# Moving the single tile from the front of a row of blocks of three to its end (LayerNorm, affine and tanh-GELU on 8192 x 2048)

## The chip, the cores and the metric

One core of one Trainium2 chip. The metric is the device time of one execution in microseconds (us). A profile gives the span from the first to the last instruction, which is 1.7 us shorter than the time of the same execution (317.9 against 319.62 us in the kernel before).

## The reference

```python
def reference(x, gamma, beta, eps):            # x: 8 x 1024 x 2048, float32
    mean = np.mean(x, axis=-1, keepdims=True)
    var = np.var(x, axis=-1, keepdims=True)
    out = gamma * (x - mean) / np.sqrt(var + eps) + beta
    return 0.5 * out * (1 + np.tanh(np.sqrt(2 / np.pi) * (out + 0.044715 * out ** 3)))
```

The 8192 rows are 64 tiles of 128 rows; a tile is 1.049 MB. Each is read once and written once.

## The kernel before

64 is one more than 3 x 21. The kernel loads and stores tiles in blocks of three (3.1 MB a transfer) and computes their scales in groups of three, so a single tile has to stand somewhere. It stands at the front, as block 0 and group 0. Blocks decide the transfers, groups decide the order of statistics; in the code they are two separate lists.

```python
    R = 3; NB = 7                                  # tiles in a block, block buffers
    starts = [0] + list(range(1, ntiles, R))       # blocks: 1, 3, 3, ...
    ...
    def load(b):
        xt = xin.tile([P, R, d], F32, name="xt")   # always room for three tiles
        ...                                        # blocks 0 and 1: one DMA a tile; then one DMA a block
    for b in range(NB):
        load(b)                                    # seven blocks ahead, from SyncE's queue
    ...
    groups = [1] + [3] * ((ntiles - 1) // 3)       # first tile of each group of three: statistics on ScalarE,
    ...                                            # all others on VectorE
    def gelu(j):                                   # ScalarE, in place, then the store from ScalarE's queue
        ...
        elif q == dst.shape[1] - 1:                # last tile of its block (last three blocks: each tile by itself)
            nc.scalar.dma_start(out=dst, in_=blocks[b][:, :dst.shape[1], :])
            if b + NB < len(starts):
                load(b + NB)                       # into the buffer that this store frees
```

The other steps: per tile VectorE writes (x - mean) * gamma into PSUM (line 166), PE adds beta times the standard deviation (line 169), ScalarE takes the Gelu with the scale 1/std (line 178). GpSimd works out the scales, once per group.

## Time and profile before

| | before |
|---|---|
| time, median (range), 3 runs | 319.86 us (319.84 to 320.2) |
| span of the profiled run | 317.9 us |
| bytes moved | 134.38 MB |
| busy: VectorE, PE, ScalarE | 84%, 80%, 76% |

VectorE has the largest share among the engines.

### The profile page before, as it was taken

The numbers are of one execution on the slowest core, as the hardware profiler recorded it, in microseconds if no ns is written. First come the engines' busy times: TensorE is split into PE (matmuls) and PEld (weight loads), VectorE is DVE, ScalarE is ACT, GpSimd is POOL, SyncE is SP. The second block draws the span as 40 slices with busy tenths as digits, with TensorE's granted clock in tenths as the row PEclk, the third lists the DMA queues.
The fourth block names the chain that finished last, engine by engine and source line by source line (L and its number), as shares of the span: only waits on it lengthen the run. The fifth ranks groups of instructions, "written<-read, shape, count | busy, mean of one in ns | idle before, by whom it ended". The sixth has DMA issues, their size and how long they took to land.

```text
span 317.9 us, 2209 instructions
## 1 busy us (share of the span) xinstructions
PE 255.8 (80%) x528; PEld 104.1 (33%) x528; DVE 266.1 (84%) x344; ACT 242.6 (76%) x282; POOL 91.2 (29%) x181
## 2 busy tenths in 40 slices
PE   5987979978989889789789895777979595979920
PEld 2322434323433333333233332332423232424400
DVE  2678889999999999999999979797979879797600
ACT  2365989998898988988988969587787769685720
POOL 0203324414225144043142250404234150506000
PEclk9997979999999999999999999979799998979985
DMA  7999999999999999999999999999999999999996
GB/s 292 436 442 442 387 438 422 428 429 430 436 431 433 430 433 433 427 436 431 427 433 439 430 430 432 433 431 436 424 436 433 436 425 433 430 439 409 426 429 265
DMA packets 7649, 134.38 MB, mean 423 GB/s; under 512 B 850, under 2 KB 850, under 8 KB 1106
## 3 DMA queue, kind: packets, MB, share of 16 engines
q1 hardware_dynamic: 3456, 67.11, 49.5%
q10 hardware_dynamic: 4180, 67.13, 49.3%
q8 instruction: 4, 0.07, 0.1%
q14 instruction: 9, 0.07, 0.1%
HBM read 67.13 MB, written 67.11 MB: 422 GB/s over the span
## 4 chain that ended last, share of the span: by engine, by line
DMA 42%; DVE 31%; issue 9%; POOL 5%; PE 4%; ACT 4%; ACTq 0%; POOLq 0%; DVEq 0%; SPq 0%
DMA out_dram<-xt 26%; DVE ps L166 17%; DMA xt<-in_x_dram 16%; DVE st L125 13%; PE ps L169 4%; ACT xt L178 3%; DVE mv L127 1%; POOL y L149 1%; ACT w L160 1%; POOL t L152 1%; ACT junk L131 1%; POOL ve L148 1%; POOL t L151 1%; POOL y L153 1%; POOL t L150 0%
## 5 line engine op out<-in xcount | busy, mean ns | idle before, releaser
L169 PE MATMUL ps<-b_t,w 128*128 128x512 f32 x512 | 241.8, 626 | 44.4 <-DVE ps L166 38.9
L166 DVE SCALAR_TENSOR_TENSOR ps<-xt,mv,g_t 128x1024 f32<-128x1024 f32 x128 | 156.2, 1265 | 7.0 <-ACT xt L178 6.9
L169 PEld LDWEIGHTS ps<-b_t,w 128*128 128x128 f32 x512 | 99.0, 199 | 188.0 <-issue 102.3
L178 ACT ACTIVATE xt<-ps,y 128x1024 f32<-128x1024 f32 x128 | 137.3, 1104 | 25.9 <-PE ps L169 24.9
L125 DVE BATCH_NORM_STATS2 st<-xt 128x6 f32<-128x512 f32 x172 | 107.9, 680 | 23.3 <-DMA xt<-in_x_dram 23.3
L138 POOL TENSOR_SCALAR mv<-sq 128x1 f32<-128x1 f32 x21 | 8.7, 416 | 144.5 <-ACT junk L136 144.5
L136 ACT ACTIVATE junk<-xt,mv 128x2048 fp8e5<-128x2048 f32 x21 | 42.0, 2002 | 8.0 <-ACT xt L178 8.0
L131 ACT ACTIVATE junk<-xt 128x2048 fp8e5<-128x2048 f32 x21 | 40.0, 1904 | 8.4 <-DMA xt<-in_x_dram 7.9
L149 POOL TENSOR_TENSOR y<-ve,power 128x3 f32<-128x3 f32 (+1 forms) x22 | 34.7, 1577 | 1.8
L148 POOL TENSOR_SCALAR ve<-mv 128x3 f32<-128x3 f32 (+1 forms) x22 | 20.2, 918 | 45.5 <-DVE mv L127 45.3
L160 ACT ACTIVATE w<-ident,std 128x128 f32<-128x128 f32 x64 | 20.8, 388 | 7.1 <-POOL std L154 7.1
L127 DVE BATCH_NORM_AGGREGATE mv<-st 128x2 f32<-128x24 f32 x43 | 11.3, 263 | 2.7
L98 PE MATMUL ps<-g_t,ones 1*128 1x512 f32 x8 | 7.2, 1073 | 3.7 <-DMA g_t<-in_gamma_dram 3.7
L101 ACT ACTIVATE g_t<-ps 128x1024 f32<-128x1024 f32 x2 | 2.0, 1023 | 6.7 <-PE ps L98 6.7
L98 PE MATMUL ps<-b_t,ones 1*128 1x512 f32 x8 | 7.0, 1056 | 0.0
L152 POOL TENSOR_SCALAR t<-t 128x3 f32<-128x3 f32 (+1 forms) x22 | 6.3, 287 | 1.9
L151 POOL TENSOR_TENSOR t<-t,ve 128x3 f32<-128x3 f32 (+1 forms) x22 | 6.1, 276 | 1.7
L153 POOL TENSOR_TENSOR y<-y,t 128x3 f32<-128x3 f32 (+1 forms) x22 | 5.2, 235 | 1.8
L101 ACT ACTIVATE b_t<-ps 128x1024 f32<-128x1024 f32 x2 | 2.0, 1023 | 4.8 <-PE ps L98 4.8
L150 POOL TENSOR_TENSOR t<-y 128x3 f32<-128x3 f32 (+1 forms) x22 | 5.1, 234 | 1.7
L154 POOL TENSOR_TENSOR std<-ve,y 128x3 f32<-128x3 f32 (+1 forms) x22 | 4.3, 194 | 1.7
L98 PEld LDWEIGHTS ps<-g_t,ones 1*128 1x128 f32 x8 | 2.5, 325 | 6.8 <-issue 6.8
(12 smaller groups left out, 13.0 us busy)
## 6 DMA issues: line engine op xcount, KB each, us to landing
xt<-in_x_dram SPq DMA_DIRECT2D x20, 3072.0 KB, 22.5
out_dram<-xt ACTq DMA_DIRECT2D x18, 3072.0 KB, 34.9
out_dram<-xt ACTq DMA_DIRECT2D x9, 1024.0 KB, 18.3
xt<-in_x_dram SPq DMA_DIRECT2D x4, 1024.0 KB, 8.6
out_dram<-xt ACTq DMA_DIRECT2D x2, 512.0 KB, 12.1
g_t<-in_gamma_dram ACTq DMA_DIRECT2D x1, 8.0 KB
b_t<-in_beta_dram ACTq DMA_DIRECT2D x1, 8.0 KB
```

The source lines that it names most:

```text
L98: nc.tensor.matmul(pt[:, c:c + BANK], lhsT=ones[0:1, :], rhs=row[0:1, s.start + c:s.start + c + BANK], start=True, stop=True)
L125: nc.vector.bn_stats(out=sts[i][:, c, :], in_=xts[i][:, c * BANK:(c + 1) * BANK])
L127: nc.vector.bn_aggr(out=slot(i), in_=sts.pop(i))
L131: nc.scalar.activation(out=junk, in_=xts[i], func=ACTF.Identity, scale=-1.0 / d, accum_out=slot(i)[:, 0:1], saturate=False)
L136: nc.scalar.activation(out=junk, in_=xts[i], func=ACTF.Square, bias=slot(i)[:, 0:1], accum_out=sq, saturate=False)
L148: po.tensor_scalar(out=ve, in0=mvs[g][:, :, 1], scalar1=float(eps), scalar2=None, op0=ADD)
L149: po.tensor_tensor(out=y, in0=ve, in1=power[:, :m], op=mybir.AluOpType.pow)
L152: po.tensor_scalar(out=t, in0=t, scalar1=-0.5, scalar2=1.5, op0=MUL, op1=ADD)
L160: nc.scalar.activation(out=w, in_=ident, func=ACTF.Identity, scale=rstds[g][1][:, k:k + 1])
L166: nc.vector.scalar_tensor_tensor(out=pt, in0=xts[j][:, s], scalar=mvs[g][:, k, 0:1], in1=g_t[:, s], op0=ADD if j in on_scalar else SUB, op ...
L169: nc.tensor.matmul(pt[:, c:c + BANK], lhsT=wts[j], rhs=b_t[:, s.start + c:s.start + c + BANK], start=False, stop=True, skip_group_check=True)
L178: nc.scalar.activation(out=xts[j][:, s], in_=pt, func=ACTF.Gelu_apprx_tanh, scale=rstds[g][0][:, k:k + 1])
```

## The change

The intent: the row of blocks starts with full blocks of three and the single tile closes it; the groups likewise. The first loads ahead are then full buffers, and the last group is short.

```diff
-    starts = [0] + list(range(1, ntiles, R))
+    starts = list(range(0, ntiles, R))
...
-        m = R if i else 1
+        m = min(R, ntiles - i)
...
-            nc.sync.dma_start(out=xt, in_=src)
+            nc.sync.dma_start(out=xt[:, :m, :], in_=src)
...
-    groups = [1] + [3] * ((ntiles - 1) // 3)
+    groups = [3] * (ntiles // 3) + [1] * (ntiles % 3)
```

## The prediction

> **What bounds the kernel now.** I read the page from the top (busy shares, then the 40 slices), then the table of stretches, then the chain that ended last, then the single DMA issues. The 64 tiles are 128 rows of 2048 floats, 1.049 MB each way, so 128 tile transfers in all. The shares alone do not decide it: VectorE 84%, PE 80%, ScalarE 76%. The slices do:
>
> ```profile
> DVE  2678889999999999999999979797979879797600
> ...
> DMA  7999999999999999999999999999999999999996
> GB/s 292 436 442 442 387 438 422 428 429 430 436 431 433 430 433 433 427 436 431 427 433 439 430 430 432 433 431 436 424 436 433 436 425 433 430 439 409 426 429 265
> ```
>
> VectorE is full only from slice 6 to about slice 21 and has holes after that; the DMA row stands at 9 from the second slice to the last but one. A table of seven stretches that I cut at the events of the run (first store issued at 30.2, second at 44.5 and landed at 65.6, last load landed at 276.9, last store issued at 305.1; the last two columns are DMA share and GB/s) says the same in numbers:
>
> ```profile
> 0.00:30.20 30.20, 23.18 (x28) 8.83 (x29) 18.49 (x29) 12.84 (x16) 5.75 (x21) 0.97 0.95 399
> 30.20:44.50 14.30, 12.24 (x24) 5.05 (x23) 12.57 (x17) 12.87 (x15) 4.20 (x8) 0.86 1.00 415
> 44.50:65.60 21.10, 20.33 (x46) 8.33 (x44) 19.66 (x27) 19.42 (x23) 8.10 (x16) 0.98 1.01 426
> 65.60:138.00 72.40, 62.38 (x140) 25.51 (x140) 71.67 (x93) 64.10 (x76) 22.89 (x43) 1.00 1.00 432
> 138.00:276.90 138.90, 113.11 (x244) 46.29 (x243) 123.82 (x160) 112.36 (x131) 44.26 (x86) 0.96 1.00 432
> 276.90:305.10 28.20, 24.58 (x53) 10.14 (x51) 19.90 (x22) 20.98 (x24) 5.96 (x9) 0.94 1.00 425
> 305.10:317.90 12.80, 0.00 (x0) 0.00 (x0) 0.00 (x0) 0.00 (x0) 0.00 (x0) 0.62 0.78 328
> ```
>
> From these the span can be rebuilt. The page counts 134.38 MB; at 432 GB/s that is 311.1 us. What each stretch loses against 432: (432-399)/432 x 30.2 = 2.3 us at the start, 0.6 and 0.3 in the next two, none in the two long ones, 0.5 in the sixth, (432-328)/432 x 12.8 = 3.1 at the end. 311.1 + 6.8 = 317.9 us, the span to a tenth. The timed 319.86 us is 2.0 us more, outside the span. So the whole time is bytes, a start-up, and a drain; in the last 12.8 us no engine computes at all.
>
> The chain of waits must be read with this in mind. In the middle it runs along VectorE at 12.47 us for three tiles; near 133 us it leaves it, and then hops from store to load:
>
> ```profile
> 143.14 38.55 DMA out_dram<-xt
> 181.71 0.03 issue
> 181.74 22.47 DMA xt<-in_x_dram
> ...
> 209.48 44.87 DMA out_dram<-xt
> 254.37 0.03 SPq L70
> 254.40 0.03 issue
> 254.43 22.49 DMA xt<-in_x_dram
> ```
>
> A store of three tiles takes 45 us to land although its bytes need only 7.3 us at 432 GB/s: it stands behind two other stores and shares with the loads. A buffer comes free only then, and SyncE issues the next load within 0.1 us. The VectorE stretch is therefore no bound of the end: VectorE goes faster (12.47 us per three tiles) than the transfers can follow (2 x 3 x 1.049 MB / 432 GB/s = 14.6 us), and only piles up stores. The last step of the chain is ScalarE at 303.96 us, 14 us before the span ends, which is the drain again.
>
> **What the Trainium skill says.** "DMA: Bandwidth & Descriptors", section Specifications, gives 435 GB/s as the ceiling of the fabric and about 358 GB/s as a limit per core on the HBM side. The trace agrees with the first: 432 GB/s over 211 us. It contradicts the second for this run; "HBM Reference", section Specifications (TRN2), says why that may be: a core that streams alone is measured well above the share, at about 425 GB/s. Either way the transfers are at the ceiling. The section Issuing engines are not separate DMA queues of the first page says that transfers from ScalarE's and SyncE's queues run on the same 16 engines and interleave. The trace agrees: a three-tile load lands in 22.5 us with stores beside it, and in 7.3 us after the one before it when loads run alone (below). So what one queue does not use the other gets, and order alone takes no byte away.
>
> **The change part by part.** No instruction of weight is added or removed: 64 tiles, 43 with VectorE statistics, 21 with ScalarE's. The group of one goes from tile 0 to tile 63, and all other groups shift by one tile. Five effects:
>
> 1. Loads at the start. Blocks 0 and 1 are now both of three, so six single-tile loads instead of four, and the seven buffers take 21 tiles ahead instead of 19. Cost of issue: 0.44 us each (median), two more singles, against a queue that holds tens of us of work: 0 on the path.
>
> 2. The first tiles on the engines. Before, tile 0 is alone: statistics at 6.07, scale chain done at 11.18, stored at 30.17. After, tile 0 is one that ScalarE must pass over twice. ScalarE is free at 18.7 (the four evictions of gamma and beta), mean to 20.9, variance to 23.0; GpSimd's chain takes it to 27.1 (the trace has exactly this, for tile 1), diagonals to 28.1. This is the place that the first group of three, tiles 1 to 3, has now. It stores at 44.49. Without the Gelu of tile 0 in between, but with the next group's mean moved into the gap and a cold PE at the first matmuls, I get 43 to 45 for the store of tiles 0 to 2. So store k after stands where store k+1 stood before: compute is one tile behind, 12.47/3 = 4.2 us.
>
> 3. The first recycling. Before, the one-tile block's store frees a whole buffer and the eighth load goes out at 45.53. After, it waits for the first three-tile store. Single loads land at 13.80 (4 tiles), 21.12 (7), 28.42 (10): 2.44 us a tile. At 44.5, pure loads have brought 4 + 30.7/2.44 = 16.6 tiles; 4.4 are left, and with the three of the store 7.4 x 2.44 = 18.0 us of work, to 62.5. The second store (about 56.7) adds three tiles, to 69.8. The first store lands by 62.5 plus up to 2 or 3 us (the very first load took 5.26 us for 2.4 us of bytes), the eighth load is issued at 63 to 66 and moves by 68. The third store is issued at about 68.3. The queue is thus never empty, with 2 to 7 us to spare: cost 0, and a bubble of a few us if I am off.
>
> 4. The steady stretch: the same bytes at 432 GB/s. Loads issued later land later, but are needed later too; VectorE has 2.1 us per group in hand.
>
> 5. The end. All 64 loads are through by about 277 as before (the halves of the traffic stay equal), but the last is of one tile and the last group's chain is of one element per partition (2.25 us for tile 0 at the start, against 5.6 us for the last group now). From 277: statistics to 280, then four tiles at about 3.5 us of matmul, so the last Gelu near 295 to 300 in place of 305.1. At that time the queue holds more, 15 to 20 us of stores against 11.9. Stores also reuse eight completion counters in turn, so the last can't go out before the one eight earlier has landed; that one is the last three-tile store, at about 300. All this is under the drain: gain 0.
>
> Sum: 311.1 + 2.3 + 0.9 + 0.5 + 3.1 = 317.9 as before, plus an expected 0.1 us for part 3, plus 2.0 outside: 319.9 us.
>
> **Rivals.**
> (a) The bubble. The eighth load goes out some 18 us later; if the first store took 25 us to land rather than 18 to 21, and the second came late as well, the DMA row would show a hole near 62 to 70 and the time would be 321 to 324. For it: the one-tile store at 30.2 needed 15.3 us until the load that waits for it went out, so stores behind a queue of loads are slow. Against it: whatever makes the store slow is loads that move.
> (b) Compute bounds: then being one tile later at the front costs 4.2 us, 324. For it: the chain runs 85 us along VectorE. Against it: the DMA row, and 12.8 us of drain.
> (c) The tail bounds: an earlier last group would give up to 5 to 8 us, 312 to 315. For it: the chain ends in GpSimd, PE and ScalarE of the last group. Against it: 11.9 us between the last issue and its landing, in which the rate is 423 to 430 GB/s until 312.
> (d) A more even drain: in the last 4 us the rate falls to 203 and 16 GB/s. Other stores at the end could make this better or worse by 1 us.
>
> **Range and chances.** The core of the sum is bytes over a rate that neither part touches. (a) in a mild form and (d) make the spread: 318.5 to 322.0 us. 2% are 6.4 us: faster would need (c), slower (a) and (b) together. Faster 0.01, within 0.95, slower 0.04.
>
> **What would show it.** Right: the DMA row at 9 throughout, 134.38 MB, 432 GB/s in the middle; the first store, of 3072 KB, at 43 to 45; the eighth block's load at 63 to 66; the last store issued before 303 and more than 12 us in flight. Wrong: a slice of 7 or less near 60 to 72 (a); ScalarE's last Gelu within 5 us of the end (b); a span shortened by the amount that the last Gelu moves (c). The prediction as a whole falls if the rate in the middle is not 430 to 433, for which I see no reason.

## The result, and the profile after

| | before | after |
|---|---|---|
| time, median (range), 6 runs each | 320.2 us (319.84 to 320.26) | 320.3 us (319.98 to 320.85) |
| ratio, 95% interval | | 1.0009 (0.9996 to 1.0021) |
| span of the profiled run | 317.9 us | 318.3 us |
| first store issued | 30.17 us, one tile | 45.85 us, three tiles |
| load of the eighth block issued | 45.53 us | 62.95 us |
| last store issued | 305.11 us | 303.67 us |

A ratio here and below is the mean time of one kernel's fast runs over that of the other's of the same rounds, so not quite the ratio of the medians quoted. The times are the same within the noise: the interval contains 1.

First the slices of the changed kernel. The first store is 16 us later, yet the DMA row has no hole: 9 from the second slice to the last but one.

```profile
DVE  0675688999999999999999999999797979899300
...
DMA  7999999999999999999999999999999999999995
```

Then the same seven stretches (columns as in the prediction: busy time and count of PE, weight load, VectorE, ScalarE and GpSimd, the granted clock, DMA share, GB/s).

```profile
0.00:30.20 30.20, 16.09 (x19) 6.15 (x20) 15.74 (x25) 12.12 (x14) 5.04 (x14) 1.00 0.96 398
30.20:44.50 14.30, 12.59 (x25) 5.17 (x25) 9.35 (x12) 10.09 (x14) 4.30 (x8) 1.00 0.99 423
44.50:65.60 21.10, 18.97 (x43) 7.73 (x42) 19.48 (x25) 19.34 (x22) 8.31 (x13) 1.00 1.01 428
65.60:138.00 72.40, 62.38 (x140) 25.22 (x138) 71.58 (x94) 64.61 (x77) 22.25 (x45) 1.00 1.00 431
138.00:276.90 138.90, 115.58 (x252) 47.33 (x251) 129.72 (x168) 117.57 (x138) 44.66 (x87) 0.97 1.00 432
276.90:305.10 28.20, 25.34 (x56) 10.60 (x54) 19.99 (x23) 18.73 (x20) 11.37 (x15) 0.95 1.00 425
305.10:318.30 13.20, 0.00 (x0) 0.00 (x0) 0.00 (x0) 0.00 (x0) 0.00 (x0) 0.57 0.74 309
```

In the first 30.2 us VectorE works 15.7 us instead of 18.5 and PE 16.1 instead of 23.2: compute really starts later. The last column hardly moves. Against 432 GB/s the changed kernel loses 0.4 us less than before in the two stretches from 30.2 to 65.6, 0.2 us more from there to 138, and 0.7 us more in the last one, where no engine computes in either kernel.

The most telling place is 60 to 64 us. These are the two queues there (SyncE's loads are q1, ScalarE's stores q10; packets, each one piece of a transfer that one DMA engine moves, MB, share of the 16 engines), in the kernel before and then after.

```profile
q1 hardware_dynamic: 40, 0.98, 57.0%
q10 hardware_dynamic: 43, 0.69, 40.2%
```

```profile
q10 hardware_dynamic: 83, 1.65, 95.8%
q1 hardware_dynamic: 1, 0.00, 0.0%
```

After the change the loads ahead are used up at 60 us and the next load is not yet on its way. The loads stand still. The stores that are waiting take their place at once, and the sum of the two queues (1.67 and 1.65 MB) is the same.

Last, the shares of the chain that ended last. In the kernel before:

```profile
DMA 42%; DVE 31%; issue 9%; POOL 5%; PE 4%; ACT 4%; ACTq 0%; POOLq 0%; DVEq 0%; SPq 0%
```

and after:

```profile
DVE 51%; DMA 20%; issue 12%; PE 6%; ACT 3%; POOL 3%; ACTq 0%; DVEq 0%; POOLq 0%; SPq 0%
```

From "mostly DMA" to "mostly VectorE", at equal time. The chain follows back from the last Gelu, and the last Gelu does not end the kernel: it ends 13 to 15 us before the span does. What moved is the place where the chain leaves VectorE for a store and the load behind it (near 133 us before, near 197 after), not a bound. The traces also show when the compute has used up its stock of loaded tiles: from 30 us on, VectorE waits for no load until 189.69 us before and 228.03 us after; from then on it waits some 2 us for a load in every group, and the groups come every 14.5 us, the pace of the transfers, in place of 12.47.

### The profile page after: what moved, and what is told of

Same layout as the page of the kernel before. It is cut to its first block, busy times and chain, and to the rows that moved or that the text cites. A ratio compares the mean times of both kernels' runs of the same rounds, so it can differ in the third digit from the quotient of the medians.

```text
span 318.3 us, 2212 instructions
## 1 busy us (share of the span) xinstructions
PE 251.0 (79%) x528; PEld 102.2 (32%) x528; DVE 265.8 (84%) x344; ACT 242.5 (76%) x282; POOL 95.9 (30%) x181
## 2 busy tenths in 40 slices
DMA packets 7649, 134.38 MB, mean 422 GB/s; under 512 B 850, under 2 KB 850, under 8 KB 1106
## 4 chain that ended last, share of the span: by engine, by line
DVE 51%; DMA 20%; issue 12%; PE 6%; ACT 3%; POOL 3%; ACTq 0%; DVEq 0%; POOLq 0%; SPq 0%
DVE ps L166 29%; DVE st L125 20%; DMA out_dram<-xt 13%; DMA xt<-in_x_dram 7%; PE ps L169 6%; DVE mv L127 2%; ACT xt L178 2%; POOL t L151 1%; POOL t L152 1%; ACT junk L131 1%; POOL y L149 1%; ACT w L160 0%; POOL mv L138 0%; POOL ve L148 0%; POOL y L153 0%
## 5 line engine op out<-in xcount | busy, mean ns | idle before, releaser
L169 PE MATMUL ps<-b_t,w 128*128 128x512 f32 x512 | 237.0, 616 | 48.1 <-DVE ps L166 35.7
L169 PEld LDWEIGHTS ps<-b_t,w 128*128 128x128 f32 x512 | 97.1, 195 | 188.7 <-issue 97.8
L149 POOL TENSOR_TENSOR y<-ve,power 128x3 f32<-128x3 f32 (+1 forms) x22 | 35.6, 1616 | 1.8
L148 POOL TENSOR_SCALAR ve<-mv 128x3 f32<-128x3 f32 (+1 forms) x22 | 21.1, 959 | 38.8 <-DVE mv L127 38.5
L151 POOL TENSOR_TENSOR t<-t,ve 128x3 f32<-128x3 f32 (+1 forms) x22 | 8.2, 375 | 1.7
L152 POOL TENSOR_SCALAR t<-t 128x3 f32<-128x3 f32 (+1 forms) x22 | 7.1, 321 | 1.9
L154 POOL TENSOR_TENSOR std<-ve,y 128x3 f32<-128x3 f32 (+1 forms) x22 | 5.2, 238 | 1.7
L153 POOL TENSOR_TENSOR y<-y,t 128x3 f32<-128x3 f32 (+1 forms) x22 | 4.3, 194 | 1.8
```

Of the source, the lines that this page charges most:

```text
L148: po.tensor_scalar(out=ve, in0=mvs[g][:, :, 1], scalar1=float(eps), scalar2=None, op0=ADD)
L149: po.tensor_tensor(out=y, in0=ve, in1=power[:, :m], op=mybir.AluOpType.pow)
L151: po.tensor_tensor(out=t, in0=t, in1=ve, op=MUL)
L169: nc.tensor.matmul(pt[:, c:c + BANK], lhsT=wts[j], rhs=b_t[:, s.start + c:s.start + c + BANK], start=False, stop=True, skip_group_check=True)
```

## The experiments

**Theory D**: the transfers bound. Their queue is never empty, so neither the later start nor the earlier end of the compute reaches the end of the kernel. **Rival C**: the compute sets the end; it loses at the front and wins at the tail by about as much. Both give a ratio of 1, so the result alone does not tell them apart.

| kernel | median us | ratio to before | 95% interval |
|---|---|---|---|
| blocks_only | 320.06 | 1.0006 | 0.9991 to 1.0020 |
| groups_only | 319.92 | 1.0000 | 0.9985 to 1.0015 |
| after_tail4 | 320.22 | 1.0004 | 0.9988 to 1.0021 |
| after_tail10 | 329.16 | 1.0284 | 1.0263 to 1.0306 |
| after_copy | 318.15 | 0.9941 | 0.9927 to 0.9956 |
| before_half | 293.20 | 0.9159 | 0.9145 to 0.9173 |
| after_half | 297.79 | 0.9307 | 0.9290 to 0.9325 |
| before_six | 322.36 | 1.0078 | 1.0063 to 1.0093 |
| after_six | 323.36 | 1.0111 | 1.0094 to 1.0128 |
| before_front | 327.45 | 1.0240 | 1.0221 to 1.0259 |
| after_front | 332.23 | 1.0386 | 1.0368 to 1.0403 |

Each was run four times, beside seven runs of the kernel before on the same chip, in three rounds on three chips: the kernel before had a median of 319.96 us beside blocks_only, groups_only and the two with six buffers, 319.99 beside the two tails, the copy and before_half, and 319.69 beside after_half and the two fronts. Results are correct but for the copy and the two halves. Their outputs are wrong, which doesn't matter for the times.

### Each half of the change alone

In the changed kernel (blocks_only), and in the kernel before (groups_only):

```diff
 # blocks_only
-    groups = [3] * (ntiles // 3) + [1] * (ntiles % 3)
+    groups = [1] + [3] * ((ntiles - 1) // 3)
 # groups_only
-    groups = [1] + [3] * ((ntiles - 1) // 3)
+    groups = [3] * (ntiles // 3) + [1] * (ntiles % 3)
```

> The blocks of loads and stores as in the changed kernel (3 x 21, then 1), the groups of statistics as before (1, then 3 x 21). Theory D (the transfers bound, their queue is never empty, order of compute does not reach the end): ratio 0.998 to 1.004, no hole in the DMA row. Rival C (compute sets the end; a loss of about 4 us at the front and a gain of about 4 us at the tail happen to cancel): this kernel keeps the early first tile and the late last group of three, so it should differ from groups_only by some us, one of the two above 1.006.

> The groups as in the changed kernel, the blocks as before; the other half of the change. D: ratio 0.998 to 1.004. C: one of blocks_only and groups_only slower by 2 us or more and the other faster by as much.

Both are the same as before, within 0.2%. If a loss and a gain cancelled between the two lists, these kernels would have shown them apart. A loss and a gain that both come from the list of groups (a later first tile, an earlier last group) would still cancel in groups_only, so these two do not refute C by themselves; the runs below do. The first three-tile store goes out at 37.49 us in blocks_only (its first block holds the early tile 0 and two tiles of the next group) and the last store at 309.83 us; both moments moved by 6 to 8 us against the changed kernel and the span (318.2 us) did not.

### A later end of the compute

In the changed kernel, K = 4 or 10 passes of ScalarE over a row of 2048, for nothing, ahead of the last tile's Gelu:

```diff
+    for _ in range(K):
+        nc.scalar.activation(out=junk, in_=b_t, func=ACTF.Identity, saturate=False)
     gelu(ntiles - 1)
```

> The changed kernel with four extra ScalarE passes (1.9 us each, 7.6 us) right before the last tile's Gelu. The last store was issued at 303.7 and landed at 317.4, so by D a store issued at about 311 still finds other stores ahead of it until 314.9: time within 0.5 us of the changed kernel, ratio to before 0.999 to 1.004. C: 7.6 us more, ratio 1.024.

> Ten such passes, 19 us: last store issued at about 322.7, when the queue has been empty since about 315. D: the span ends about 4 us after that issue, near 326.5, so 8 to 10 us over the changed kernel, not 19 (ratio to before 1.025 to 1.033). C: 19 us more, ratio 1.06.

Four passes put the last store's issue from 303.67 to 311.79 us and cost nothing. Ten put it at 324.37. The stretches of after_tail10 show when the queue gave out (columns as above):

```profile
303.00:309.00 6.00, 1.24 (x3) 0.19 (x1) 0.00 (x0) 5.90 (x4) 0.00 (x0) 0.96 1.01 429
309.00:315.00 6.00, 0.00 (x0) 0.00 (x0) 0.00 (x0) 5.91 (x4) 0.00 (x0) 0.50 0.62 264
315.00:322.00 7.00, 0.00 (x0) 0.00 (x0) 0.00 (x0) 6.91 (x5) 0.00 (x0) 0.50 0.00 0
322.00:328.00 6.00, 0.00 (x0) 0.00 (x0) 0.00 (x0) 1.87 (x2) 0.00 (x0) 0.50 0.44 175
```

The last issue moved by 20.7 us and the span by 9.6 (318.3 to 327.9), so 11.1 us were absorbed. This is the slack at the tail, good to about 1 us (the four runs of after_tail10 spread from 328.43 to 329.75). It is what the last store stood behind: in the changed kernel it took 13.7 us from issue to landing, in after_tail10, into an empty queue, 2.6. That difference is the same measurement said in another way, not a second one. C, which expects 7.6 and 19 us, falls for the tail.

### The transfers without the compute

```diff
-            nc.scalar.activation(out=xts[j][:, s], in_=pt, func=ACTF.Gelu_apprx_tanh,
-                                 scale=rstds[g][0][:, k:k + 1])
+            nc.scalar.activation(out=xts[j][:, s], in_=xts[j][:, s], func=ACTF.Gelu_apprx_tanh)
...
-    (the loop over statistics, scales, affine and Gelu)
+    for j in range(ntiles - 1):
+        gelu(j)
```

> The changed kernel's loads and stores with the compute taken away: only the in-place Gelu of the raw input stays (wrong result on purpose). D: the floor of these transfers, 317 to 320 us against 320.2, so compute costs at most 3 us. C: VectorE's work gone, the time should fall well below, 300 or less.

With all work of VectorE, PE and GpSimd on the tiles gone the time falls by 0.6%, to 318.15 us. The transfers, with one pass of ScalarE between a tile's load and its store, need 99.4% of the time. Two stretches of it, VectorE at nothing and the rate as in the whole kernel:

```profile
30.20:138.00 107.80, 0.00 (x0) 0.00 (x0) 0.00 (x0) 40.20 (x42) 0.00 (x0) 1.00 1.00 432
138.00:276.90 138.90, 0.00 (x0) 0.00 (x0) 0.00 (x0) 61.85 (x64) 0.00 (x0) 1.00 1.00 432
```

### The same change where the transfers do not bound

Only the left half of each tile is stored, in both kernels:

```diff
-            if j == ntiles - 1:
+            if j == ntiles - 1 and h == 0:
...
-                nc.scalar.dma_start(out=dst[:, q, :], in_=xts[j])
+                nc.scalar.dma_start(out=dst[:, q, :H], in_=xts[j][:, :H])
...
-            nc.scalar.dma_start(out=dst, in_=blocks[b][:, :dst.shape[1], :])
+            nc.scalar.dma_start(out=dst[:, :, :H], in_=blocks[b][:, :dst.shape[1], :H])
```

> The kernel before with only the left half of each tile stored (half of the output is left unwritten, wrong on purpose): 100.8 MB in place of 134.4, some 233 us at 432 GB/s, so the transfers no longer bound. D: compute bounds, VectorE at 12.47 us per group of three all the way; last group's store near 294 to 300, time 298 to 306. C: also shorter, as stores come free sooner; says nothing by itself, see after_half.

> The changed kernel with half of each tile stored, to set beside before_half. D: where compute bounds, the cost of the change that the transfers hide must show. One tile later from the front on is 4.2 us, less 1 to 3 us for a last group of one: 1 to 5 us more than before_half. C (front loss and tail gain cancel along compute): equal to before_half within 1 us.

Here the change costs 4.6 us (293.20 to 297.79; the two ran in different rounds on different chips, but the ratios to the kernel before say the same: 0.9307 - 0.9159 = 0.0148, 4.7 us of 320). The long middle stretch shows what bounds (before_half first, then after_half):

```profile
90.00:252.10 162.10, 140.47 (x312) 57.13 (x312) 160.32 (x209) 142.64 (x170) 59.79 (x104) 1.00 0.90 359
```

```profile
90.00:252.10 162.10, 140.38 (x313) 57.08 (x312) 160.31 (x209) 142.64 (x170) 59.72 (x104) 1.00 0.90 354
```

VectorE is busy 160.3 of 162.1 us and the transfers have room. After_half's first four stores go out 0.9 us later than before_half's stores 2 to 5, with one tile less done (12.47/3 = 4.2 us), so the compute is 5.1 us behind at the front; its last store goes out 4.55 us later, so the shorter last group gives back only half a microsecond. So the cost of the change to the compute is real. D expected it to be 1 to 5 us; C expected equality. The absolute time of before_half was a miss: 298 to 306 us expected, 293.20 measured. The drain was right (4 to 6 us from the last store's issue to the end expected, 5.3 measured); the last store itself went out at 287.93 and not at 294 to 300, as the compute was ahead of 12.47 us per group counted from the kernel before's second store: that store came at 43.10 in place of 44.49, the third 10.76 us after it, and the last one, which needs only the left half of the last tile, some 3 us before that pace.

### Less slack at the front: six buffers

```diff
-    NB = 7
+    NB = 6
```

> The changed kernel with six block buffers in place of seven. By D the hidden cost of the change is the later first recycling. 18 tiles are loaded ahead, through at 47.7 us; the first store goes out at 45.9 and has landed at about 56.5, the second is issued at 57.2: the queue is empty from 55 to 58.5. Expected 3 to 5 us over before (ratio 1.009 to 1.016), a hole in the DMA row near 55 to 59 us. C: no change against the seven buffers but what a slower steady stretch costs both kernels alike.

> The kernel before with six block buffers. 16 tiles ahead, through at 43 us, with the first one-tile store 45.5; that store frees a buffer at 43 to 45 and the second store goes out at 44.5, so the queue is nearly never empty. D: 0 to 1.5 us over before (ratio 1.000 to 1.005), so 2 to 5 us less than after_six. C: the same as after_six.

The changed kernel did as expected (3.4 us over before). The hole is there, shorter and earlier than expected: next to no packet starts from 54 to 56 us, where 55 to 58.5 had been put, with a first store at 44.67 and not at 45.9. It is the second of these stretches (after_six). Share and GB/s count a packet where it starts, so in stretches as short as these a share can pass 1.00 and a rate can jump by some per cent.

```profile
44.00:52.00 8.00, 7.66 (x19) 3.25 (x18) 6.79 (x9) 7.54 (x8) 3.75 (x8) 1.00 1.00 430
52.00:56.00 4.00, 2.60 (x6) 0.88 (x6) 3.97 (x6) 3.97 (x7) 0.00 (x0) 1.00 0.33 139
56.00:60.00 4.00, 3.59 (x9) 1.44 (x8) 4.00 (x6) 3.59 (x4) 1.37 (x1) 1.00 1.00 313
60.00:64.00 4.00, 4.00 (x10) 1.71 (x9) 3.96 (x6) 3.14 (x4) 2.90 (x3) 1.00 0.96 375
```

The kernel before was a miss: 2.4 us over, not 0 to 1.5, and so only 1.0 us better than after_six. Its stretches:

```profile
44.00:52.00 8.00, 8.00 (x17) 3.40 (x17) 6.80 (x9) 6.88 (x8) 3.75 (x8) 0.87 0.92 348
52.00:56.00 4.00, 3.63 (x9) 1.44 (x8) 3.90 (x6) 4.00 (x7) 0.00 (x0) 1.00 0.91 393
56.00:60.00 4.00, 3.60 (x9) 1.33 (x8) 4.00 (x6) 3.58 (x5) 0.58 (x1) 1.00 1.12 428
60.00:64.00 4.00, 4.00 (x11) 1.81 (x10) 3.96 (x7) 3.83 (x5) 3.05 (x4) 1.00 0.92 363
```

The early one-tile store does free its buffer early (the next load goes out at 45.10 us, against 55.20 in after_six). But the single tile also takes a buffer with room for three, so only 16 tiles are ahead instead of 18, and they end just as that load is issued: 348 GB/s from 44 to 52 lose 1.6 us, 393 from 52 to 56 and 363 from 60 to 64 together 1.0. The early store and the smaller stock nearly offset each other. The expectation had counted both (16 tiles through at 43 us, the load issued at 43 to 45) and called the queue nearly never empty. What it left out is the start of new transfers: the second store was issued at 44.38 us, its packets move from 45.3, which makes 213 GB/s from 44 to 46, and with the load behind it the rate stays at 393 from 46 to 52.

### Less slack at the front: a later first store

In both kernels, eight passes of ScalarE (15.5 us) ahead of the first mean:

```diff
     junk = singles.tile([P, d], mybir.dt.float8e5)
+    for _ in range(8):
+        nc.scalar.activation(out=junk, in_=b_t, func=ACTF.Identity, saturate=False)
```

> The changed kernel with eight extra ScalarE passes (15.5 us) before the first mean, so that the first stores come 15.5 us later. Loads ahead (21 tiles) are through at 55.0; first store at 61.3, second at 72.7. D: the queue is empty from 55 to 63 and again for about 2 us near 70: 8 to 11 us over the changed kernel, ratio to before 1.025 to 1.036. C: 15.5 us more (1.048).

> The same eight passes in the kernel before. First one-tile store at 45.7, so the next load goes out at 52 to 54 while the 19 tiles ahead and this store keep the queue until 52.9; second store at 60. D: empty for 1 to 2 us near 53 and 1 to 3 near 69: 2 to 5 us over before, ratio 1.006 to 1.016, and 4 to 8 us less than after_front. C: 15.5 us more, as after_front.

In the changed kernel the first store went from 45.85 to 60.06 us (14.2 later) and the span from 318.3 to 329.4 (11.1 longer): 3.1 us were absorbed. In the kernel before, 30.17 to 44.77 (14.6) and 317.9 to 325.6 (7.7): 6.9 us. These are the slacks at the front, for this one delay. The 3.1 is good to about 1 us, so 2 to 4.5: the first store of the changed kernel came at 44.41 to 44.73 us in three other runs with the same compute at the front, and the profiled execution of after_front was the fastest of its four. For the changed kernel three stretches (after_front): a dead queue until the first store, and a second hole before the first recycled load (issued at 70.06 us). Together they lose 9.5 us.

```profile
52.00:56.00 4.00, 3.79 (x9) 1.33 (x7) 3.97 (x7) 3.96 (x5) 3.44 (x6) 1.00 0.42 178
56.00:60.00 4.00, 2.50 (x6) 1.25 (x7) 3.13 (x5) 2.96 (x5) 0.85 (x3) 1.00 0.00 0
...
68.00:72.00 4.00, 2.60 (x7) 1.01 (x6) 3.96 (x6) 3.55 (x8) 0.00 (x0) 1.00 0.33 90
```

and for the kernel before (before_front) the same:

```profile
52.00:56.00 4.00, 1.29 (x4) 0.22 (x2) 3.96 (x6) 3.09 (x4) 3.59 (x6) 1.00 0.39 117
56.00:60.00 4.00, 3.46 (x5) 1.43 (x6) 3.42 (x5) 3.46 (x6) 0.05 (x1) 0.69 0.94 393
```

The difference between the two (4.8 us) came as expected; the sizes did not. I expected 8 to 11 us over the changed kernel and 2 to 5 over the kernel before and got, by the ratios, 12.1 and 7.7. In the kernel before, 2.9 us are the hole at 52 to 56 us; the rest is spread: 1.2 us between 44 and 52 (368 GB/s), 1.9 between 60 and 72 (367 and 352), 1.6 between 72 and 90 (396 and 392). Part of that is at a DMA share of 1.00, as in after_six from 56 to 60 (313 GB/s). There the packets themselves take longer: 51 packets of 24,576 bytes, all of loads, take as much time as the 16 engines have in those 4 us, 1.26 us each, where a packet of this size takes 0.91 us in the long stretches. On a smaller scale it is there without a hole: from 48 to 49 us in the changed kernel, some 2 us after its first store was issued, 16 packets of the loads take 1.16 us each. The expectations had not charged for this; what slows the packets is not settled by these runs.

No version that beats both kernels was found: the copy of the changed kernel's transfers is only 0.6% below the kernel before, and nothing was tried on the transfers themselves.

## Why the prediction was right

319.9 us was predicted and 320.3 measured, within 318.5 to 322.0, and "within 2%" had 0.95. By its own steps:

- **Bytes over a rate.** 134.38 MB again, 431 and 432 GB/s in the two long stretches. The sum rebuilt from the stretches after (311.1 plus losses of 2.4, 0.3, 0.2, 0.2, 0, 0.5 and 3.8) is 318.5 against a span of 318.3. Held, and the copy shows it independently. One slip: the 2.0 us outside the span set the span of one execution (319.62 us) beside the median of others (319.86); for one and the same execution it is 1.7.
- **The first tiles (part 2).** First store at 43 to 45 us expected, 45.85 in this profile; 44.41 and 44.73 in the profiles of after_tail10 and after_tail4, whose front is the same. In the profile by which it is judged this missed by 0.85 us, within the spread of such moments. "Store k after stands where store k+1 stood before" was a little short: the first four stores came 0.5 to 1.4 us later than that, so the compute is about 5 us behind at the front and not 4.2; at the end of after_half 4.6 are left.
- **The first recycling (part 3).** The load of the eighth block was to go out at 63 to 66 us, and went at 62.95. The spare was put at 2 to 7 us; after_front measures some 3. The queue of loads was empty for a while and the stores filled in, as argued. Held.
- **The end (part 5): gain 0 held, the moment did not.** "The last Gelu near 295 to 300" was 303.63 at its end, and the mark "the last store issued before 303" failed by 0.7 us. The step that failed is "From 277: statistics to 280". The last load was not through by 277 us: its last packets moved at 280, one tile in some 16 us beside the stores. And the last tile's statistics came only at 284.39 us, without a wait for it: VectorE was still busy with the affine steps of the group before. And the last group's scale chain was sized at 2.25 us from tile 0; it took 7.4 (287.32 to 294.71). The likely reason is in the Trainium skill, which I did not use here: by "SBUF — State Buffer", section SBUF: two separate sides, a VectorE instruction with two SBUF inputs and a GpSimd instruction that reads SBUF shut each other out. Four of the seven one-element steps of GpSimd took 1.11 to 1.16 us beside VectorE's affine steps (two SBUF inputs, 1.27 us each), and one took 0.19 us in the 0.2 us gap between two of them; for the group before, beside VectorE's statistics (one SBUF input), the last five steps took 0.19 to 0.20 us each (285.28 to 286.57). This is inferred from the durations, no run isolated it. Neither reached the path: behind them PE ran 13.98 us without a gap, and behind that stood the drain. 15 to 20 us of stores were expected in the queue at the last issue, and the last store took 13.7 us to land.
- **Rivals.** The bubble (a) did not occur with seven buffers but is real: six buffers or a later start bring it. (b), compute bounds, is refuted by after_copy, and shows when half the stores are dropped. (c), the tail bounds, is refuted by after_tail4. (d) is the most that may be left: the last stretch loses 3.8 us instead of 3.1. With the small differences before it that makes the 0.4 us of span, which is within the run-to-run spread of the changed kernel (0.9 us) and was not followed further.

## What to carry to other kernels

When the DMA row is full from start to end, reorder for the transfers' sake only: ask when the first buffer comes back and how many bytes are queued until then, and measure the slack at both ends by putting idle work there. A change that the transfers hide is not free: this one costs the compute 4.6 us and takes the slack at the front from some 7 to some 3 us, and it comes due with fewer buffers (1.0 us with six) or fewer bytes (4.6 us with half of the stores). The chain of waits named VectorE for half of a span that VectorE did not bound; check where the chain ends before believing its shares, and how long the engine waits for loads once its stock is used up.

## What the Trainium skill lacked or had wrong

- "DMA: Bandwidth & Descriptors", section Specifications, puts the HBM side at about 358 GB/s per core. A core alone, loading and storing at once, held 432 GB/s for over 200 us, just under the page's fabric ceiling of 435. The exception for a core alone stands elsewhere ("HBM Reference", section Specifications (TRN2), about 425 GB/s) and is a little below what was measured here.
- "DMA: Bandwidth & Descriptors", section Queues, rings and completion order, has the engines take turns between queues packet by packet. The trace agrees: between 34.5 and 44.7 us in the kernel before, the one-tile store moved its 128 packets of 8,192 bytes while the loads ahead moved 140 of 24,576. The page does not spell out what follows when packets differ in size: the queue with the small packets gets the small share, so a small early store is slow to free its buffer (15.4 us from its issue to the load that waits for it).
- No page says that packets can take longer for a few microseconds when transfers start in a queue that stood empty. In after_six, right after the hole, the share stood at 1.00 for 4 us at 313 GB/s, with 1.26 us per packet of 24,576 bytes in place of 0.91.
